# The first three channel chunks of a two-layer trunk kernel, taken together by pairs of k tiles

## The chip, the cores and the metric

One NeuronCore of one Trainium2 chip runs the whole program. The metric is the device time of one execution in microseconds. The kernel before takes 932.64 us (median of 3 runs, 932.36 to 933.33).

## What is computed

A decoder trunk of two layers over 256 positions and a model width of 1024, all in float32. The change touches only the opening of the first layer: an RMS norm and the first columns of one wide projection.

```python
h = rms_norm(x, norm_mix_g[i])          # x * rsqrt(mean(x*x) + 1e-6) * g
proj = h @ w_in                          # 1024 x 7960
(z, xbc, dt_raw, r_q, ...) = jnp.split(proj, idx, axis=-1)
xbc = jax.nn.silu(causal_dwconv(xbc, ssm_conv_w, ssm_conv_b))
...                                      # three token mixers, gates, w_out, then a gated MLP
```

## The kernel before

Float32 products are made of three rounded products: every weight and every activation is split into a high part and a low part, and TensorE adds high x high, high x low and low x high. A weight arrives in pieces of 128 partitions (`piece`, L167): a DMA on SyncE's queue into one of 4 `raw` buffers (L176), a cast on ScalarE that gives the high part `whi` (L183), a subtraction on VectorE that gives the low part `wlo` (L184). There are 6 buffers each of `whi` and `wlo`. Pieces are asked for 5 ahead of their use (`LOOK`); the dictionary `before` holds work that is put ahead of a given piece.

The activation is x itself, transposed, in 8 k tiles of 128 channels by 256 positions. It is loaded in 4 pairs of k tiles (`FirstNorm.ahead`, L340), each pair put ahead of one of pieces 1 to 4. ScalarE multiplies a k tile by the norm's gain and rounds it (`slot_h`, L302), VectorE makes the rest (`slot_l`, L303). The norm's other factor, one over the root mean square of each position, is not needed for the matmuls; it is multiplied in afterwards. It is made as follows: ScalarE squares the pairs (L348), GpSimd adds them up (L350, L354), TensorE sums over partitions (L358), VectorE takes the inverse root by 11 small operations (`rsqrt`, L284 to L289) and spreads it on a diagonal (L319), TensorE turns that into a row for all partitions (L322), ScalarE copies it out as `r_bc` (L324).

The first layer's matmuls start with three channel chunks of `xbc` of 256 columns each (chunks 2, 0, 1), each with 8 k tiles and 6 matmuls for a k tile, so 48 matmuls a chunk. Chunks 2 and 0 run interleaved (`chan_two`, in the order `LATE`), then chunk 1 (`chan_major`), then 16 matmuls of a narrow chunk (`narrow`, L256 and L260), then `z` (`tok_major`, L274 to L276). The results lie in PSUM tiles `mm`, of which there are 4. Each is freed when VectorE has multiplied it by `r_bc`: L459 in `take_xbc` for a channel chunk, L475 in `take_small` for the narrow one. `z` needs two `mm` tiles.

Ahead of all this, 5 matmuls of ones (`WARM`, L1065, 10 passes) keep TensorE at work while nothing has been loaded.

The order on each engine is that of a planner which follows the program's order of priority as far as its own estimate of readiness lets it; the queues then run in that fixed order. Side work (`spawn`) is advanced after a given number of `yield`s of the main stream, by the constants `N` and `W`.

Of the kernel before, what the change touches and what calls it, by code (L numbers as in the profile page):

```python
# [9 lines left out]
F32 = mybir.dt.float32  # L10
# [3 lines left out]
ALU = mybir.AluOpType  # L14
# [3 lines left out]
P = 128  # L18
D = 1024
T = 256  # L20
L = 2
KT = D // P
# [12 lines left out]

WARM = 5

LATE = (0, 2, 8, 10, 4, 12, 6, 14)

N = (3, 8, 3, 5, 3, 2)  # L40

# [13 lines left out]
PO = {}  # L55
_at = 0
# [6 lines left out]
PIECE = 1024  # L63
FIRST = 512
REST = 9
X_AT = 40
NFIRST = 2
RAW_BUFS = 4
# [51 lines left out]
for _l in range(L):  # L120
    for _n, (_kind, _j, _w) in enumerate(PLAN):
        _step = FIRST if _l == 0 and _n < NFIRST else PIECE
        PIECE_AT[_l, _kind, _j] = len(PIECES), _step
        PIECES += [(_l, _n, _o, min(_step, _w - _o)) for _o in range(0, _w, _step)]


@with_exitstack
def hybrid_trunk(ctx: ExitStack, tc: tile.TileContext, xT_in, x_in, wall, par, wa2, cst, phase, dret, fin, gbias, out):
    nc = tc.nc
# [9 lines left out]
    xt = cpool.tile([P, 2, D], F32, name="xt")  # L139
    params = [cpool.tile([P, NP], F32, name=f"par{l}") for l in range(L)]  # L140
    cs = cpool.tile([P, NC_CONST], F32, name="cs")
    ident = cs[:, CO_ID:CO_ID + P]
# [45 lines left out]
    def weight(l, kind, idx, k, cols):  # L188

        o = k * cols  # L190
        p, step = PIECE_AT[l, kind, idx]
        c = slice(o % step, o % step + cols)
        return (a[:, c] for a in piece(p + o // step))

# [54 lines left out]
    def narrow(l, act):  # L249

        ah, al = act
        acc = mm_tile()
        both = piece(PIECE_AT[l, "small", 0][0])[0].rearrange("p (k c) -> p k c", c=P)
# [73 lines left out]
    class FirstNorm(Norm):  # L327
# [9 lines left out]
        def ahead(self, j):  # L337
            o = 2 * (j % 2)
            x = self.x[j // 2][:, o:o + 2, :]
            nc.sync.dma_start(x, xT_in[:, 2 * j:2 * j + 2, :])  # L340
            for i in range(2):
                k = 2 * j + i
                split_scaled(self.slot[0][:, k, :], self.slot[1][:, k, :], x[:, i, :], self.g[:, k:k + 1])

        def square(self, j):
            sq = self.acc if j == 0 else t_main()
            o = 2 * (j % 2)
            nc.scalar.activation(two(sq), self.x[j // 2][:, o:o + 2, :], AF.Square)  # L348
# [557 lines left out]
    def layer(l, norm):  # L906

        mx = Mixers(l, norm)
        x_act = slots[0]
# [7 lines left out]

        yield from chan_two(l, "xbc", (2, 0), x_act, take)
        acc = yield from chan_major(l, "xbc", 1, x_act)
        mx.take_xbc(1, acc)  # L920
        yield
        mx.take_small(narrow(l, x_act))
        ssm = spawn(mx.ssm(), 1)
# [135 lines left out]
    def stream():  # L1059
        norm = FirstNorm(params[0][:, PO["mix_g"]:PO["mix_g"] + 8], slots[0])  # L1060

# [4 lines left out]

        def rest_ahead():
# [4 lines left out]
            for j in range(4):  # L1072
                norm.square(j)
# [18 lines left out]
def _lay_weights(i):  # L1092
# [4 lines left out]
    def put(l, kind, j, w):  # L1097
        k = w.shape[0] // P
        w = w.reshape(k, P, -1).transpose(1, 0, 2).reshape(P, -1)
        p, step = PIECE_AT[l, kind, j]  # L1100
        for o in range(0, w.shape[1], step):
            wall[p + o // step, :, :min(step, w.shape[1] - o)] = w[:, o:o + step]

# [102 lines left out]
```

## Time and profile before

| | before |
|---|---|
| time of 3 runs, us | 932.64 (932.36 to 933.33) |
| time of the profiled execution, us | 932.3 |
| its span from first to last instruction, us | 930.5 |
| TensorE matmul busy in it | 914.5 us, 98% |
| VectorE busy | 712.9 us, 77% |
| ScalarE busy | 506.8 us, 54% |

The span leaves out 1.8 us that lie around the instructions. Times in the rows are microseconds from the start of the span. A busy TensorE is not TensorE at its peak: it counts as busy at half clock as well, and the ends of matmuls are modelled, so the distance between the starts of two matmuls says more than the duration of one.

### The profile page before, as it was taken

To read this page: it belongs to the slowest core of one execution; us is meant where nothing else is said; L and a number is where in the kernel's file an instruction comes from. 1 tells how busy PE (TensorE), PEld (TensorE's weight loads), DVE (VectorE), ACT (ScalarE), POOL (GpSimd) and SP (SyncE) were. 2 spreads that over 40 slices of the span, in tenths; PEclk is the share of its full clock that TensorE was granted. 3 is DMA by queue.
4 is the path that set the end of the run, shared out by engine and by line. 5 is a ranking of instruction groups with operands and counts; after the bars stand their busy time and mean duration, and the time that the engine had idled before them with its cause. 6 is when DMAs were issued, how large, how long until landed. Compare 5 with 4: busy or idle time off the path is not lost.

```text
span 930.5 us, 14996 instructions
## 1 busy us (share of the span) xinstructions
PE 914.5 (98%) x5726; PEld 816.1 (88%) x5726; DVE 712.9 (77%) x1111; ACT 506.8 (54%) x748; POOL 78.4 (8%) x74
## 2 busy tenths in 40 slices
PE   8999999999999999999999999999999999999995
PEld 7879889888889999999898898888888999999994
DVE  6976888576768887787799578777667697777775
ACT  6765454454456555555566635554545575555552
POOL 3032200003200000000002131000120000000001
PEclk9999999999999999999999999999999999999998
DMA  7775655556655656555466556444665566555531
GB/s 255 276 243 166 219 172 170 152 162 210 201 181 161 202 183 186 188 192 181 147 186 183 198 168 218 158 139 156 206 212 194 169 188 189 190 183 184 183 109 46
DMA packets 51288, 169.94 MB, mean 183 GB/s; under 512 B 5968, under 2 KB 8336, under 8 KB 51088
## 3 DMA queue, kind: packets, MB, share of 16 engines
q1 hardware_dynamic: 50928, 168.46, 56.3%
q8 instruction: 45, 0.74, 0.3%
q10 hardware_dynamic: 288, 0.52, 0.2%
q14 instruction: 27, 0.22, 0.1%
HBM read 165.81 MB, written 1.05 MB: 179 GB/s over the span
## 4 chain that ended last, share of the span: by engine, by line
PE 94%; DVE 3%; ACT 1%; DMA 1%; issue 0%; SPq 0%; ACTq 0%
PE mm L227 13%; PE mm L228 13%; PE mm L229 13%; PE mm L274 12%; PE mm L275 12%; PE mm L276 12%; PE mx L1025 4%; PE mx L1024 4%; PE mx L1026 4%; PE mx L555 2%; DVE wlo L184 1%; PE mx L558 1%; DVE xbc L466 1%; PE mx L542 1%; DMA x_t<-x_t 1%; PE mx L726 1%
## 5 line engine op out<-in xcount | busy, mean ns | idle before, releaser
L184 DVE TENSOR_TENSOR wlo<-raw,whi 128x1024 fp32r<-128x1024 f32 (+1 forms) x300 | 377.6, 1261 | 123.6 <-ACT whi L183 120.6
L183 ACT CAST whi<-raw 128x1024 fp32r<-128x1024 f32 (+1 forms) x302 | 311.7, 1034 | 266.4 <-PE mm L276 109.3
L227 PE MATMUL mm<-slot_h,whi 128*128 128x256 f32 x992 | 282.4, 285 | 2.2 <-ACT slot_h L302 2.2
L228 PE MATMUL mm<-slot_l,whi 128*128 128x256 f32 x992 | 281.5, 284 | 0.1
L229 PE MATMUL mm<-slot_h,wlo 128*128 128x256 f32 x992 | 281.5, 284 | 0.0
L274 PE MATMUL mm<-whi,slot_h 128*128 128x512 f32 x512 | 203.9, 398 | 0.0
L275 PE MATMUL mm<-wlo,slot_h 128*128 128x512 f32 x512 | 200.4, 391 | 0.0
L276 PE MATMUL mm<-whi,slot_l 128*128 128x512 f32 x512 | 200.3, 391 | 0.0
L227 PEld LDWEIGHTS mm<-slot_h,whi 128*128 128x128 f32 x992 | 190.5, 192 | 4.9 <-ACT slot_h L302 2.6
L228 PEld LDWEIGHTS mm<-slot_l,whi 128*128 128x128 f32 x992 | 190.7, 192 | 2.1 <-DVE slot_l L303 0.3
L229 PEld LDWEIGHTS mm<-slot_h,wlo 128*128 128x128 f32 x992 | 190.7, 192 | 0.1
L274 PEld LDWEIGHTS mm<-whi,slot_h 128*128 128x128 f32 x512 | 96.2, 188 | 20.6 <-issue 0.7
L276 PEld LDWEIGHTS mm<-whi,slot_l 128*128 128x128 f32 x512 | 96.1, 188 | 20.3
L275 PEld LDWEIGHTS mm<-wlo,slot_h 128*128 128x128 f32 x512 | 96.3, 188 | 18.7
L1014 DVE SCALAR_TENSOR_TENSOR tm<-tm,par 128x255 f32<-128x255 f32 (+1 forms) x176 | 73.6, 478 | 0.7 <-ACT tm L1012 0.7
L1024 PE MATMUL mx<-whi,slot_h 128*128 128x512 f32 x176 | 69.1, 392 | 0.0
L1025 PE MATMUL mx<-wlo,slot_h 128*128 128x512 f32 x176 | 69.0, 392 | 0.0
L1026 PE MATMUL mx<-whi,slot_l 128*128 128x512 f32 x176 | 68.5, 389 | 0.0
L1012 ACT ACTIVATE tm<-tm,par 128x256 f32<-128x256 f32 x88 | 48.0, 592 | 4.3 <-DVE tm L1007 4.3
L1007 DVE TENSOR_TENSOR tm<-mm,r_bc 128x512 f32<-128x512 f32 x44 | 30.4, 690 | 23.1 <-PE mm L229 23.1
L1018 ACT CAST slot_h<-tm 128x256 fp32r<-128x256 f32 x44 | 17.9, 406 | 49.1 <-DVE tm L1017 49.0
L1026 PEld LDWEIGHTS mx<-whi,slot_l 128*128 128x128 f32 x176 | 33.1, 188 | 7.1
(193 smaller groups left out, 758.6 us busy)
## 6 DMA issues: line engine op xcount, KB each, us to landing
raw<-w_all SPq DMA_DIRECT2D x292, 512.0 KB, 3.5
gate_b<-gate_b SPq DMA_DIRECT2D x12, 256.0 KB, 3.5
st<-ret_decay SPq DMA_DIRECT2D x8, 384.0 KB, 3.8
raw<-w_all SPq DMA_DIRECT2D x10, 256.0 KB, 3.9
x_t<-x_t SPq DMA_DIRECT2D x4, 256.0 KB, 5.8
xt<-x_tok SPq DMA_DIRECT2D x1, 1024.0 KB, 6.3
r_c<-q SPq DMA_DIRECT2D x16, 64.0 KB, 2.0
r_d<-q SPq DMA_DIRECT2D x16, 64.0 KB, 2.0
```

What stands on the lines that cost most here:

```text
L183: nc.scalar.copy(h_out, r_in)
L184: nc.vector.tensor_tensor(l_out, r_in, h_out.bitcast(F32), ALU.subtract)
L227: nc.tensor.matmul(o, lhsT=wh[:, c], rhs=ah[:, k, :], start=first, stop=False)
L228: nc.tensor.matmul(o, lhsT=wh[:, c], rhs=al[:, k, :], start=False, stop=False)
L229: nc.tensor.matmul(o, lhsT=wl[:, c], rhs=ah[:, k, :], start=False, stop=last)
L274: nc.tensor.matmul(acc[t], lhsT=ah[:, k, c], rhs=wh, start=first, stop=False)
L275: nc.tensor.matmul(acc[t], lhsT=ah[:, k, c], rhs=wl, start=False, stop=False)
L276: nc.tensor.matmul(acc[t], lhsT=al[:, k, c], rhs=wh, start=False, stop=last)
L1014: nc.vector.scalar_tensor_tensor(a[:, d:], u[:, :T - d], mx.pc("fconv_w", 3 * ct + 2 - d), a[:, d:], ALU.mult, ALU.add)
L1024: nc.tensor.matmul(o, lhsT=ah[:, a, tok], rhs=wh, start=first, stop=False)
L1025: nc.tensor.matmul(o, lhsT=ah[:, a, tok], rhs=wl, start=False, stop=False)
L1026: nc.tensor.matmul(o, lhsT=al[:, a, tok], rhs=wh, start=False, stop=last)
```

## The change

- The three channel chunks of the first layer run together. Their weights come in 12 pieces of 512 columns (a pair of k tiles each), in the order in which they are used: the first pair of k tiles of chunks 2, 0 and 1, then the second pair, and so on. Three `mm` tiles are held until all 144 matmuls and the narrow chunk are done; only then `finish(factor)`, `take_small` and `take_xbc` follow.
- The pair of k tiles 0 of x is put ahead of piece 0, on ScalarE's DMA queue; the other pairs ahead of pieces 3, 6 and 9, on SyncE's.
- The norm's gain for the first layer comes as a small array of its own (`first_g`, 8 columns) on ScalarE's queue. The layer's parameters move from the head of SyncE's queue to just ahead of piece 8, and the constants to ahead of piece 11.
- The squares are put ahead of pieces 4, 7, 10 and 12. The last addition of squares and the closing sum move from GpSimd to VectorE.
- The object `Mixers` of the first layer is made after the second pair of k tiles; `WARM` goes from 5 to 6, `N[0]` from 3 to 2, `N[3]` from 5 to 8.

```diff
-WARM = 5
+WARM = 6
-N = (3, 8, 3, 5, 3, 2)
+N = (2, 8, 3, 8, 3, 2)
-REST = 9
+REST = 13
-NFIRST = 2
+NFIRST = 3
...
+    _cuts = [(_n, _o) for _o in range(0, PLAN[0][2], FIRST) for _n in range(NFIRST)] if _l == 0 else []
+    _cuts += [(_n, _o) for _n in range(NFIRST if _l == 0 else 0, len(PLAN)) for _o in range(0, PLAN[_n][2], PIECE)]
...
-            nc.sync.dma_start(x, xT_in[:, 2 * j:2 * j + 2, :])
+            (nc.sync if j else nc.scalar).dma_start(x, xT_in[:, 2 * j:2 * j + 2, :])
...
-                nc.gpsimd.tensor_tensor(self.acc, self.acc, sq, ALU.add)
+                (nc.vector if j == 3 else nc.gpsimd).tensor_tensor(self.acc, self.acc, sq, ALU.add)
...
-            nc.gpsimd.tensor_tensor(s1, self.acc[:, :T], self.acc[:, T:], ALU.add)
+            nc.vector.tensor_tensor(s1, self.acc[:, :T], self.acc[:, T:], ALU.add)
...
+            acc = [mm_tile() for _ in range(3)]
+            for k in range(0, KT, 2):
+                for i, b in enumerate((2, 0, 1)):
+                    chan_steps(l, "xbc", b, x_act, acc[i], (k, k + 1))
+                    yield
+                if k == 2:
+                    mx = Mixers(l, norm)
+            small = narrow(l, x_act)
+            yield
+            finish(factor)
+            mx.take_small(small)
+            for i, b in enumerate((2, 0, 1)):
+                mx.take_xbc(b, acc[i])
...
-        before.update({q + 1: lambda j=q: norm.ahead(j) for q in range(4)})
-        before[REST] = rest_ahead
-        nc.sync.dma_start(params[0], par[0])
+        before.update({3 * q: lambda j=q: norm.ahead(j) for q in range(4)})
+        before.update({3 * q + (4 if q < 3 else 3): lambda j=q: norm.square(j) for q in range(4)})
+        before[8] = lambda: nc.sync.dma_start(params[0], par[0])
+        before[11] = constants
+        before[REST] = rest_ahead
+        nc.scalar.dma_start(first_g, fg)
```

## Rows read from the trace of the kernel before

**Rows 1.** The page: busy time, share of the span, instructions of two engines.
```profile
PE 914.5 (98%) x5726; PEld 816.1 (88%) x5726; DVE 712.9 (77%) x1111; ACT 506.8 (54%) x748; POOL 78.4 (8%) x74
```
**Rows 2.** All waits of TensorE in the span: us in total, times, longest us.
```profile
PE mm L227 <- ACT slot_h L302: 2.2, 1, 2.2
...
PE mx L593 <- DVE da L584: 0.8, 1, 0.8
```
**Rows 3.** Instructions of TensorE in order of time: start us, us, line, what.
```profile
1.10 4.14 PE L1065 MATMUL mx<-ones 128*128 128x256 f32 x10 [1.10 <-POOL ones L150]
7.40 0.38 PE L227 MATMUL mm<-slot_h,whi 128*128 128x256 f32 x1 [2.16 <-ACT slot_h L302]
...
8.24 0.41 PE L229 MATMUL mm<-slot_h,wlo 128*128 128x256 f32 x1
...
11.44 0.28 PE L229 MATMUL mm<-slot_h,wlo 128*128 128x256 f32 x1
```
**Rows 4.** Busy us of each engine in three stretches, granted clock, DMA share, GB/s.
```profile
4.59:8.00 3.41, 1.11 (x5) 0.46 (x3) 1.31 (x3) 1.16 (x3) 0.00 (x0) 1.00 0.87 278
8.00:11.42 3.42, 3.42 (x16) 3.42 (x17) 3.21 (x7) 3.42 (x9) 0.00 (x0) 0.50 0.92 327
51.50:54.90 3.40, 2.69 (x12) 1.88 (x11) 3.36 (x4) 2.12 (x3) 1.90 (x1) 1.00 0.94 311
```
**Rows 5.** DMA issues of SyncE's queue in order of time.
```profile
0.74 0.39 SPq L1080 DMA_DIRECT2D par<-params  x1
1.18 0.42 SPq L176 DMA_DIRECT2D raw<-w_all  x1
1.64 0.43 SPq L340 DMA_DIRECT2D x_t<-x_t  x1
```
**Rows 6.** Issue to landing of the first x_t, then of the first raw (0 to 2).
```profile
DMA to landing us min/median/max: 5.2/5.2/5.2
DMA to landing us min/median/max: 2.7/2.7/2.7
```
**Rows 7.** Instructions of ScalarE in order of time.
```profile
0.74 1.28 ACT L441 ACT_TABLE_LOAD   x1 [0.74 <-PEq L1198]
3.94 0.62 ACT L183 CAST whi<-raw 128x512 fp32r<-128x512 f32 x1 [0.79 <-DMA raw<-w_all]
6.84 0.91 ACT L302 ACTIVATE slot_h<-x_t,par 128x256 fp32r<-128x256 f32 x2 [2.28 <-DMA x_t<-x_t]
25.80 0.37 ACT L324 COPY r_bc<-mx 128x256 f32<-128x256 f32 x1 [1.73 <-PE mx L322]
```
**Rows 8.** Instructions of TensorE from the norm's sum to z.
```profile
19.47 0.50 PE L358 MATMUL mx<-ones,sq 128*128 128x1 f32 x4
...
25.18 0.59 PE L322 MATMUL mx<-dg,ones 128*128 128x256 f32 x2
...
25.72 0.28 PE L227 MATMUL mm<-slot_h,whi 128*128 128x256 f32 x1
...
27.52 0.28 PE L260 MATMUL mm<-slot_h,whi 128*128 128x256 f32 x1
...
29.38 0.40 PE L274 MATMUL mm<-whi,slot_h 128*128 128x512 f32 x1
```
**Rows 9.** Instructions of VectorE in the same stretch and after it.
```profile
22.63 1.23 DVE L184 TENSOR_TENSOR wlo<-raw,whi 128x1024 fp32r<-128x1024 f32 x1
...
24.44 0.48 DVE L319 TENSOR_SCALAR dg<-cs,rs_y 128x128 f32<-128x128 f32 x2
...
26.21 0.69 DVE L459 TENSOR_TENSOR tm<-mm,r_bc 128x512 f32<-128x512 f32 x1 [0.16 <-ACT r_bc L324]
...
37.64 0.41 DVE L475 TENSOR_TENSOR small<-mm,r_bc 128x256 f32<-128x256 f32 x1
```
**Rows 10.** Instructions of GpSimd: the squares added up, and their closing sum.
```profile
13.37 4.75 POOL L350 TENSOR_TENSOR sqacc<-sqacc,tm 128x512 f32<-128x512 f32 x3 [10.07 <-ACT tm L348]
18.20 1.07 POOL L354 TENSOR_TENSOR sq<-sqacc 128x256 f32<-128x256 f32 x1
```

More of the change, by code (lines that the diff above doesn't have):

```diff
@@ L121, with hybrid_trunk @@
     for _n, (_kind, _j, _w) in enumerate(PLAN):
-        _step = FIRST if _l == 0 and _n < NFIRST else PIECE
-        PIECE_AT[_l, _kind, _j] = len(PIECES), _step
-        PIECES += [(_l, _n, _o, min(_step, _w - _o)) for _o in range(0, _w, _step)]
+        PIECE_AT[_l, _kind, _j] = [], FIRST if _l == 0 and _n < NFIRST else PIECE
+    _cuts = [(_n, _o) for _o in range(0, PLAN[0][2], FIRST) for _n in range(NFIRST)] if _l == 0 else []
+    _cuts += [(_n, _o) for _n in range(NFIRST if _l == 0 else 0, len(PLAN)) for _o in range(0, PLAN[_n][2], PIECE)]
+    for _n, _o in _cuts:
+        _kind, _j, _w = PLAN[_n]
+        _at, _step = PIECE_AT[_l, _kind, _j]
+        _at.append(len(PIECES))
+        PIECES.append((_l, _n, _o, min(_step, _w - _o)))
 @with_exitstack
-def hybrid_trunk(ctx: ExitStack, tc: tile.TileContext, xT_in, x_in, wall, par, wa2, cst, phase, dret, fin, gbias, out):
+def hybrid_trunk(ctx: ExitStack, tc: tile.TileContext, xT_in, x_in, wall, fg, par, wa2, cst, phase, dret, fin, gbias, out):
     nc = tc.nc
@@ L140, in hybrid_trunk @@
     params = [cpool.tile([P, NP], F32, name=f"par{l}") for l in range(L)]
+    first_g = cpool.tile([P, KT], F32, name="first_g")
     cs = cpool.tile([P, NC_CONST], F32, name="cs")
@@ L190, in weight @@
         o = k * cols
-        p, step = PIECE_AT[l, kind, idx]
+        at, step = PIECE_AT[l, kind, idx]
         c = slice(o % step, o % step + cols)
-        return (a[:, c] for a in piece(p + o // step))
+        return (a[:, c] for a in piece(at[o // step]))
     def mm_tile():
@@ L252, in narrow @@
         acc = mm_tile()
-        both = piece(PIECE_AT[l, "small", 0][0])[0].rearrange("p (k c) -> p k c", c=P)
+        both = piece(PIECE_AT[l, "small", 0][0][0])[0].rearrange("p (k c) -> p k c", c=P)
         for k in range(KT):
@@ L906, in layer @@
     def layer(l, norm):
-        mx = Mixers(l, norm)
+        mx = Mixers(l, norm) if l else None
         x_act = slots[0]
@@ L916, in take @@
             mx.take_xbc(b, acc)
[L918 to L922, printed above, removed]
+        if l:
+            yield from chan_two(l, "xbc", (2, 0), x_act, take)
+            acc = yield from chan_major(l, "xbc", 1, x_act)
+            mx.take_xbc(1, acc)
+            yield
+            mx.take_small(narrow(l, x_act))
+        else:
+            acc = [mm_tile() for _ in range(3)]
[6 more added lines that the diff above has]
+            small = narrow(l, x_act)
+            yield
+            finish(factor)
+            mx.take_small(small)
+            for i, b in enumerate((2, 0, 1)):
+                mx.take_xbc(b, acc[i])
         ssm = spawn(mx.ssm(), 1)
@@ L1059, in stream @@
     def stream():
-        norm = FirstNorm(params[0][:, PO["mix_g"]:PO["mix_g"] + 8], slots[0])
+        norm = FirstNorm(first_g, slots[0])
         cold = mx_tile()
@@ L1065, in stream, with constants @@
             nc.tensor.matmul(cold[:, :T], lhsT=ones[:, :P], rhs=ones, start=True, stop=True)
-        def rest_ahead():
+        def constants():
             nc.sync.dma_start(cs, cst)
@@ L1071, in rest_ahead @@
                 nc.vector.tensor_tensor(o, ident[:n, :8], ident[:n, p:p + 8], ALU.add)
-            for j in range(4):
-                norm.square(j)
+        def rest_ahead():
             for l in range(1, L):
                 nc.sync.dma_start(params[l], par[l])
-        before.update({q + 1: lambda j=q: norm.ahead(j) for q in range(4)})
+        before.update({3 * q: lambda j=q: norm.ahead(j) for q in range(4)})
[3 more added lines that the diff above has]
+        before[REST] = rest_ahead
         before[X_AT] = lambda: nc.sync.dma_start(xt, x_in)
-        before[REST] = rest_ahead
-        nc.sync.dma_start(params[0], par[0])
+        nc.scalar.dma_start(first_g, fg)
         piece(0)
@@ L1099, in put @@
         w = w.reshape(k, P, -1).transpose(1, 0, 2).reshape(P, -1)
-        p, step = PIECE_AT[l, kind, j]
-        for o in range(0, w.shape[1], step):
-            wall[p + o // step, :, :min(step, w.shape[1] - o)] = w[:, o:o + step]
+        at, step = PIECE_AT[l, kind, j]
+        for p, o in zip(at, range(0, w.shape[1], step)):
+            wall[p, :, :min(step, w.shape[1] - o)] = w[:, o:o + step]
     for l in range(L):
@@ L1189 @@
         "w_all": _lay_weights(i),
+        "first_g": np.ascontiguousarray(i["norm_mix_g"][0].reshape(KT, P).T),
         "params": _lay_params(i),
```

## The prediction

> **What bounds the kernel now.** I read the engines' busy shares first, then TensorE's waits, then its instructions in order of time, and last the other engines at the places where TensorE waits. TensorE is busy for 914.5 of 930.5 us [rows 1], and the list of its waits names only two places between the first product and the last: 2.2 us before the first product, for `slot_h` on ScalarE, and 0.8 us for `da` of the first layer's SSM [rows 2]. So the end moves by what TensorE's own stream gains or loses, and the change can act only in the first 30 us. There two things cost time. One is the idle stretch: the warm-up ends at 1.10 + 4.14 = 5.24 and the first product starts at 7.40 [rows 3]. The other is not in the list of waits: the granted clock is 0.50 (1.2 instead of 2.4 GHz) from 8.00 to 11.42, after a stretch in which TensorE was busy for 1.11 of 3.41 us [rows 4]. From the start at 8.24 to the one at 11.44 there are 15 matmuls [rows 3], so 3.20 / 15 = 0.213 us each; later, from 25.72 to 27.52, 15 matmuls take 1.80 us, 0.120 each [rows 8]. The slow stretch costs 15 x 0.093 = 1.40 us.
>
> The start hangs on x. The first pair of x is issued third on SyncE's queue, at 1.64 [rows 5], and lands 5.2 us later [rows 6]; the first weights, issued at 1.18, took 2.7 and were cast at 3.94. `slot_h` starts at 6.84 [rows 7], the first product 0.56 us after that [rows 3].
>
> **The change, part by part.** The reference for the sum is the profiled execution: 932.3 us, a span of 930.5 and 1.8 around it. The median of the runs is 932.64, 0.34 above it. I take the difference from the median. What a run of this kernel can be told apart by is about 0.2%, 1.87 us.
>
> (1) First x on ScalarE's queue, parameters out of the way. `first_g` stands ahead of it there, so x is second, as the first weights were on SyncE's: issue at about 1.18 instead of 1.64. How long it takes with two queues at work, no row shows. The bounds are the two landings of rows 6: 2.7 us (landing 3.9) and 5.2 us (landing 6.4). The first product would follow 0.56 us later, at 4.5 to 6.9. It can't start before the warm-up is over: one more warm-up matmul is two passes, and two such passes cost TensorE 0.42 us at full clock (L322: from 25.18 to 25.72, less one matmul of 0.12) [rows 8], so 5.24 + 0.42 = 5.66. Before, x had the parameters and the first weights ahead of it in its one queue; now it shares only with weights, and I place the landing at 5.1, nearer to the middle of the bounds, and the first product at 5.7. Gain 7.40 - 5.7 = **1.7 us** (0.5 to 1.7). The table load on ScalarE (1.28 us, from 0.74, [rows 7]) now belongs to the first `slot_h`; behind the two DMA issues it ends by 3.0 and is hidden by x's flight. If it stood ahead of them, x would leave 1.3 us later, within the same bounds for the start.
>
> (2) The half clock. With products from 5.7 on, TensorE is idle for next to nothing between 4.59 and 8.00. In the only other stretch with an idle piece, 51.50 to 54.90, it is busy for 2.69 of 3.40 us and the clock stays at 1.00 [rows 4]. So the slow stretch goes: gain **1.4 us** (0 if x comes at the late bound: the idle time is then 6.9 - 5.66 = 1.3 us, a busy share between the two rows).
>
> (3) Three chunks together. Same 144 + 16 matmuls, fed at 3 pieces and one pair of x for 36 x 0.12 = 4.3 us: that is 1 MB, 243 GB/s, below the 327 of 8.00 to 11.42 [rows 4]. ScalarE needs 3 casts of 0.62 and 0.91 for x, and about 0.62 for a square: 3.4 us, under 4.3. VectorE's share is alike. I cost the feeding at nothing; the buffers hold some two to three pieces in hand, and a late piece would show as a wait of L227 at up to 1 us each.
>
> The price is at the end of the three chunks. Before, the norm's row (L322) ran inside chunk 1: TensorE lost only 0.42 us there, went on until 27.52, did the narrow chunk until 29.38 and found the first `mm` tile long free (L459 started at 26.21) [rows 8, 9]. Now three chunks and the narrow chunk hold all 4 `mm` tiles, and none comes free before `r_bc`. L322 stands behind the narrow chunk, and nothing else is left for TensorE. From L322's start to that of `r_bc` it is 25.80 - 25.18 = 0.62, then 0.37 for the copy [rows 7], then `take_small` 0.41 [rows 9], which comes first in the program: 0.62 + 0.37 + 0.04 + 0.41 + 0.06 = 1.50 us to `z`, if `z` may take the narrow chunk's tile. If it has to wait for the tile of chunk 2, L459's 0.69 come on top, less 0.07 of overlap: 2.11. I take 1.50, since the narrow chunk's tile is freed first. Net of the 0.42 that L322 cost before: **loss 1.1 us** (1.1 to 1.7).
>
> L322 must also be ready by then. Before, it took 25.18 - 19.47 = 5.7 us from L358 to L322 [rows 8], in which VectorE put at least two weight subtractions of up to 1.23 us between the parts of the chain [rows 9]. Now L358 stands after the tenth of twelve groups; behind it are 0.36 of its own, two groups of 1.44 and the narrow chunk's 1.86: 5.1 us of cover. With one subtraction in between I get 4.5: no wait. With two, 0.6 us (bounds 0 to 0.6). The sum of squares must be there as well: on GpSimd three additions took 4.75, 1.58 each, and the closing one 1.07 [rows 10]; the last of each go to VectorE, where a 512-column operation takes 0.69 and a 256-column one 0.41 [rows 9]. It is 1.5 us shorter, and VectorE pays 1.1 us in a stretch in which it has 2.1 of 3.41 us free at the start, 4.59 to 8.00 [rows 4]; if that cover is gone, a subtraction is 1.1 us later, and two pieces are still in hand.
>
> (4) The rest. The parameters and constants come later on SyncE's queue, each passed by weights only; `take_xbc` needs them at some 26 us, ten later than they land. Two more, smaller pieces cost SyncE two issues of 0.42. Cost nothing.
>
> (5) The wait for `da` (0.8 us, [rows 2]). VectorE takes 10 us of `take_xbc` after `r_bc`, then the SSM's chain. `r_bc` comes at about the same time as before, 5.7 + 20.2 + 0.6 = 26.5 against 25.80, but VectorE can have two or three subtractions of `z` behind it by then. Bounds: 0.8 gained to 1.3 lost; nearest to no change, taken at 0.
>
> Sum: 1.7 + 1.4 - 1.1 = 2.0 us. `z` would start at 29.38 - 2.0 = 27.4, and the time is 932.64 - 2.0 = **930.6 us** (930.3 for an execution like the profiled one).
>
> **A rule against it.** What the rows show is that x, third in its queue, took nearly twice as long as the weights two places ahead [rows 6]. The Trainium skill says under Trainium Kernel Development and Optimization, Key Constraints, that DMAs issued from SyncE's and ScalarE's queues run on the same 16 DMA engines and interleave, so that issuing from several engines saves only issue time. By that rule x would gain its place (0.46 us) and nothing more; no row here has two queues at work at the start.
>
> **The rivals.**
> - A, as above: 930.6, between 930.0 and 931.5. For it: the rows of the start. 0.42.
> - B, the norm's row or `da` costs less: the planner puts L322 among the narrow chunk, or the wait for `da` goes as well. 0.8 to 1.1 us better: 929.6 (928.7 to 930.2). 0.21.
> - C, the idle piece before `z` costs the clock. It is 1.1 to 2.3 us long; before, 2.16 us of idleness came ahead of half clock and about 0.8 us did not [rows 3, 4]. Another 1.4 us: 932.0, with the longer wait for the tile 932.6. 0.17.
> - D, x still lands 5.2 us after its issue, since HBM and not the queue is slow then. First product at 6.94: gain 0.46 of 7.40, the half clock stays, the loss before `z` stays 1.1: 933.3. With L459 and the wait for L322 (0.6 + 0.6) and a second stretch at half clock (1.4) it is 935.9. It decides from a landing after about 6.0 on: then idleness before the first product is over 0.9 us. For it: the rule above. Against it: the moved 130 KB. 0.14.
> - E, VectorE falls behind after `r_bc`, and TensorE waits longer for `da` than it does now: up to 1.3 us more, 931.9. 0.06.
>
> **How the numbers follow.** Faster by over 0.2% means under 930.77: 0.26 of A and all of B, 0.47. Slower, over 934.5: the worse part of D and a little of E, 0.09. The rest, 0.44, lies within. Range: from B's lower end to D's plain case, 928.8 to 933.4.
>
> **What would show it.** Right: the first product before 6.0, no granted clock of 0.50 up to 20 us, an idle piece of TensorE of about 1 us between L322 and L274, `z` at 27.4. Wrong: `slot_h` still waiting for x after 6, a half clock behind `z`'s start, or L227 waiting for pieces.

## The result

The changed kernel is slower: 939.94 us (938.93 to 941.35, 6 runs) against 932.32 us for the kernel before, a ratio of 1.0079 (95% interval 1.0068 to 1.0090). The forecast was 930.6 us with 933.4 as its upper end. The profiled execution of the changed kernel took 941.35 us with a span of 939.6, 9.1 us more than the 930.5 before. It was the slowest of the six; the medians are 7.6 us apart.

All of TensorE's waits after the change (us in total, times, longest us); before there were 2.2 us at the start and 0.8 us for `da` [rows 2]:

```profile
PE mx L328 <- DVE dg L325: 5.5, 1, 5.5
PE mm L280 <- DVE small L481: 3.0, 1, 3.0
PE mm L233 <- ACT slot_h L308: 1.2, 1, 1.2
PE mx L1087 <- POOL ones L156: 1.1, 1, 1.1
```

Lines have moved by 6 (by 7 in the kernels below that hold work back), that of the warm-up by 22: L328 is the norm's row (L322 before), L280 the first product of `z` (L274), L233 the first product (L227), L481 is `take_small` (L475). The two upper waits are new, the one for `da` is gone. The places in TensorE's order of time (start us, us, line, operation, idle time before it and what ended it):

```profile
1.10 4.89 PE L1087 MATMUL mx<-ones 128*128 128x256 f32 x12 [1.10 <-POOL ones L156]
7.24 0.38 PE L233 MATMUL mm<-slot_h,whi 128*128 128x256 f32 x1 [1.25 <-ACT slot_h L308]
...
25.69 0.28 PE L266 MATMUL mm<-slot_h,whi 128*128 128x256 f32 x1
...
33.23 1.22 PE L328 MATMUL mx<-dg,ones 128*128 128x256 f32 x2 [5.51 <-DVE dg L325]
...
37.48 0.80 PE L280 MATMUL mm<-whi,slot_h 128*128 128x512 f32 x1 [3.02 <-DVE small L481]
```

The first product comes at 7.24 and not at 5.7. The narrow chunk begins at 25.69 where it began at 27.52 [rows 8]: 1.83 us won. Then TensorE stands still, and `z` begins at 37.48 instead of 29.38 [rows 8]. Four stretches of TensorE (us, busy us and instructions, granted clock, DMA share, GB/s) show what the clock did:

```profile
8.00:11.40 3.40, 3.40 (x30) 1.00 1.03 352
28.00:32.00 4.00, 0.00 (x0) 1.00 0.87 294
37.48:42.80 5.32, 5.32 (x13) 0.50 0.95 369
42.80:48.12 5.32, 5.32 (x27) 1.00 0.38 128
```

The half clock behind the first product [rows 4] is gone, as forecast. A longer one has come behind the idle time: from 32.56 to 42.80 the granted clock was 0.50 (1.2 GHz), and in the first 5.32 us of `z` TensorE did 13 matmuls where it did 27 in the next 5.32 (four of these small ones of 8 columns).

**Where the 9 us are made.** VectorE from the first step of the norm to `take_small`:

```profile
23.82 0.15 DVE L290 TENSOR_SCALAR rs_v<-mx 128x2 f32<-128x2 f32 x1
25.86 1.23 DVE L190 TENSOR_TENSOR wlo<-raw,whi 128x1024 fp32r<-128x1024 f32 x1 [1.89 <-ACT whi L189]
27.00 0.16 DVE L291 TENSOR_SCALAR rs_y<-rs_v 128x2 int32<-128x2 int32 x1
...
27.39 0.16 DVE L294 SCALAR_TENSOR_TENSOR rs_a<-rs_a,rs_v 128x2 f32<-128x2 f32 x1
27.87 1.23 DVE L190 TENSOR_TENSOR wlo<-raw,whi 128x1024 fp32r<-128x1024 f32 x1 [0.32 <-ACT whi L189]
29.01 0.15 DVE L295 SCALAR_TENSOR_TENSOR rs_y<-rs_a,rs_y 128x2 f32<-128x2 f32 x1
...
29.69 1.23 DVE L190 TENSOR_TENSOR wlo<-raw,whi 128x1024 fp32r<-128x1024 f32 x1
...
31.30 1.23 DVE L190 TENSOR_TENSOR wlo<-raw,whi 128x1024 fp32r<-128x1024 f32 x1
...
32.70 0.47 DVE L325 TENSOR_SCALAR dg<-cs,rs_y 128x128 f32<-128x128 f32 x2
33.09 1.22 DVE L190 TENSOR_TENSOR wlo<-raw,whi 128x1024 fp32r<-128x1024 f32 x1
35.86 1.22 DVE L190 TENSOR_TENSOR wlo<-raw,whi 128x1024 fp32r<-128x1024 f32 x1 [1.55 <-ACT whi L189]
37.01 0.42 DVE L481 TENSOR_TENSOR small<-mm,r_bc 128x256 f32<-128x256 f32 x1
```

The steps of the norm take 0.16 us each and follow one another every 0.20 us where nothing is between them (27.00 to 27.39 holds three). Here four weight subtractions of `z`'s pieces stand between them and two more between `dg` and `take_small`. VectorE takes its instructions in the written order, so `rs_y` at 27.00, ready since 23.97, stood 3 us behind a subtraction that was itself waiting. For what, ScalarE's rows say:

```profile
24.78 1.05 ACT L189 CAST whi<-raw 128x1024 fp32r<-128x1024 f32 x1 [1.56 <-DMA raw<-w_all]
26.79 1.05 ACT L189 CAST whi<-raw 128x1024 fp32r<-128x1024 f32 x1 [0.96 <-DMA raw<-w_all]
28.61 1.04 ACT L189 CAST whi<-raw 128x1024 fp32r<-128x1024 f32 x1 [0.78 <-DMA raw<-w_all]
...
34.79 1.04 ACT L189 CAST whi<-raw 128x1024 fp32r<-128x1024 f32 x1 [2.17 <-DMA raw<-w_all]
35.74 0.37 ACT L330 COPY r_bc<-mx 128x256 f32<-128x256 f32 x1
```

Each cast waits for its weights to land. `r_bc` has no reason of its own to be late: its input was there when L328 ended (34.45 by the row above), but it stands behind the cast of 34.79, which waited for a DMA. So the order of three engines had become one line: DMA, cast, subtraction, step of the norm.

### The profile page after: what moved, and what is told of

Its sections match the earlier page's. It is cut to its first block, busy times and chain, and to the rows that moved or that the text cites. A ratio compares the mean times of both kernels' runs of the same rounds, so it can differ in the third digit from the quotient of the medians.

```text
span 939.6 us, 15017 instructions
## 1 busy us (share of the span) xinstructions
PE 917.0 (98%) x5728; PEld 817.5 (87%) x5728; DVE 712.6 (76%) x1115; ACT 507.2 (54%) x750; POOL 76.6 (8%) x72
## 4 chain that ended last, share of the span: by engine, by line
PE 94%; DMA 3%; DVE 2%; ACT 1%; issue 0%; ACTq 0%
PE mm L280 13%; PE mm L281 13%; PE mm L282 13%; PE mm L233 12%; PE mm L234 12%; PE mm L235 12%; PE mx L1046 4%; PE mx L1047 4%; PE mx L1048 4%; DMA raw<-w_all 2%; PE mx L561 2%; PE mx L564 1%; DVE wlo L190 1%; PE mx L548 1%; DMA x_t<-x_t 1%; PE mx L732 1%
## 5 line engine op out<-in xcount | busy, mean ns | idle before, releaser
L233 PE MATMUL mm<-slot_h,whi 128*128 128x256 f32 x992 | 281.9, 284 | 1.2 <-ACT slot_h L308 1.2
L280 PE MATMUL mm<-whi,slot_h 128*128 128x512 f32 x512 | 205.2, 401 | 3.0 <-DVE small L481 3.0
L233 PEld LDWEIGHTS mm<-slot_h,whi 128*128 128x128 f32 x992 | 190.0, 192 | 3.9 <-ACT slot_h L308 1.6
L280 PEld LDWEIGHTS mm<-whi,slot_h 128*128 128x128 f32 x512 | 96.9, 189 | 24.2 <-DVE small L481 3.7
```

The lines of the kernel that those rows point to most:

```text
L233: nc.tensor.matmul(o, lhsT=wh[:, c], rhs=ah[:, k, :], start=first, stop=False)
L280: nc.tensor.matmul(acc[t], lhsT=ah[:, k, c], rhs=wh, start=first, stop=False)
```

## The experiments

The theory: work that fills VectorE's and ScalarE's queues and hangs on DMAs stands in the written order ahead of the norm's steps and results; TensorE has nothing else to do, and its idle time costs the clock as well. The rivals: the norm starts too late in the new order; the supply of weights holds everything; the loss lies in the start. Ratios are to the kernel before, timed beside each, with 95% intervals.

| kernel | us | ratio |
|---|---|---|
| the change | 939.94 | 1.0079 (1.0068 to 1.0090) |
| hold_one | 936.31 | 1.0036 (1.0022 to 1.0050) |
| hold_two | 933.47 | 1.0004 (0.9995 to 1.0013) |
| start_alone | 932.64 | 0.9999 (0.9987 to 1.0011) |
| chunks_alone | 934.91 | 1.0022 (1.0011 to 1.0032) |
| warm9 | 934.29 | 1.0009 (0.9995 to 1.0022) |
| warm9_later | 940.39 | 1.0080 (1.0058 to 1.0102) |
| x_first | 933.39 | 1.0010 (0.9999 to 1.0021) |
| hold_two_x_first | 933.77 | 1.0008 (0.9998 to 1.0017) |
| stat_early | 936.22 | 1.0033 (1.0021 to 1.0045) |
| hold_two_stat_early | 933.95 | 1.0007 (0.9999 to 1.0016) |
| hold_two_da_early | 933.32 | 1.0003 (0.9992 to 1.0015) |
| da_later | 938.81 | 1.0071 (1.0046 to 1.0096) |
| pool_three | 937.62 | 1.0047 (1.0029 to 1.0064) |
| pool_six | 939.99 | 1.0074 (1.0050 to 1.0097) |
| chunks_pool | 936.61 | 1.0035 (1.0023 to 1.0048) |
| hold_two_old_start | 931.41 | 0.9977 (0.9964 to 0.9989) |

### Hold the subtractions back, in two steps

**hold_one** prepares no piece of `z` and the gates until `dg` is written.

```diff
+    cap = [13]
...
-        while len(loaded) < min(p + 1 + LOOK, len(PIECES)):
+        while len(loaded) < min(p + 1 + LOOK, len(PIECES), *cap):
...
             finish(factor)
+            cap.clear()
+            with tc.issue_after(norm.dg_made):
+                piece(12)
             mx.take_small(small)
```

> The changed kernel with one thing altered: the weight subtractions of z and of the first gate piece are traced behind the norm's chain and tied on VectorE behind its last step (L325, dg), so that none stands between the eleven steps of rsqrt. Theory (order): the fixed order of VectorE put five subtractions, each waiting for its own DMA, into the chain; without them dg is ready before the narrow chunk ends (27.6) and the wait of L328 falls from 5.5 us to under 0.5. Four casts and four subtractions now stand ahead of r_bc and of take_small instead, so z starts at 31 to 33 instead of 37.5: 933 to 937 us. Rival (weights): the weights simply come too late with the parameters and constants among them, whatever the order; then the wait moves but z still starts after 36: 938 to 941. Rival (tiles): holding all four mm tiles until r_bc is the cost in itself; then L328 is on time and z still starts some 2 us after it, 930 to 933.

VectorE from `dg` on in hold_one:

```profile
26.43 0.47 DVE L326 TENSOR_SCALAR dg<-cs,rs_y 128x128 f32<-128x128 f32 x2
26.85 2.36 DVE L191 TENSOR_TENSOR wlo<-raw,whi 128x1024 fp32r<-128x1024 f32 x2
30.38 2.48 DVE L191 TENSOR_TENSOR wlo<-raw,whi 128x1024 fp32r<-128x1024 f32 x2 [1.17 <-ACT whi L190]
32.78 0.42 DVE L482 TENSOR_TENSOR small<-mm,r_bc 128x256 f32<-128x256 f32 x1
```

`dg` comes at 26.43 instead of 32.70 and the wait for it is gone. But the four subtractions now all stand between `dg` and `take_small`: TensorE waits 4.7 us for `small`, `z` begins at 33.25, the granted clock is 0.50 from 32.99 to 36.41. The wait had moved from the first result of the norm to the second.

**hold_two** lets one piece of `z` follow `dg`, and ties the casts of the others behind `r_bc` and their subtractions behind `take_small`.

```diff
-            cap.clear()
+            cap[:] = [14]
             with tc.issue_after(norm.dg_made):
                 piece(12)
             mx.take_small(small)
+            cap.clear()
+            with tc.issue_after(norm.r_made), tc.issue_after(mx.small_made):
+                piece(12)
```

> As hold_one, and the casts of z's later pieces are tied behind r_bc on ScalarE, their subtractions behind take_small on VectorE; only z's first piece is converted earlier. Theory (order): the whole path is free, L328 starts at about 27.6, r_bc at 28.2, z at 29.0 to 29.7, against 29.38 in the kernel before; no half clock behind it: 930.5 to 933 us, level with the kernel before. Rival (weights): over 936. Rival (tiles): as the theory, with 1.4 to 2 us of idle TensorE between L328 and z left over.

TensorE in hold_two:

```profile
27.27 0.59 PE L329 MATMUL mx<-dg,ones 128*128 128x256 f32 x2
28.79 0.50 PE L281 MATMUL mm<-whi,slot_h 128*128 128x512 f32 x1 [0.92 <-DVE small L482]
```

From L329 to `z` it is 1.52 us, the 1.50 of the forecast's step (3), and `z` begins 0.6 us earlier than before the change. From 5.5 to 923 us the granted clock is 1.00. Of the 7.6 us that the change cost all but 0.7 are back (933.47 against 932.78 us of the kernel before beside it), with the start as the change has it. The first four pieces of 1024 columns land at 24.7, 26.7, 28.5 and 29.8 us in the change and at 24.5, 26.7, 28.2 and 29.5 in hold_two, the two behind them 1.4 and 1.9 us later in hold_two. `z` begins 8.7 us earlier all the same, so the supply of weights is not what held it back.

### The norm's sum two steps earlier

**stat_early** is the change with one number, `N[3]`, at 6 instead of 8; **hold_two_stat_early** is hold_two with the same. In both, and in hold_two_da_early, the sum is taken before the squares of the last two k tiles are added; they are left out of the norm.

```diff
-N = (2, 8, 3, 8, 3, 2)
+N = (2, 8, 3, 6, 3, 2)
```

> The changed kernel with one number of its schedule changed: the sum of squares and its product come two steps (two pairs of k tiles, some 2.6 us) earlier in the three chunks. VectorE's written order then has no weight subtraction among the steps of the norm, but four between dg and the product with r_bc. Theory 'subtractions that wait for their DMA stand in VectorE's order ahead of the norm's results': the wait of 5.5 us for dg goes, r_bc and the product with r_bc still stand behind four casts and four subtractions, z begins near 33 us as in hold_one (33.25), and the time is about 936 us. Rival 'the norm simply starts too late by a fixed amount': the wait for dg shrinks by 2.6 us to about 2.9 us, all else follows as before, and the time is about 937.3 us.

VectorE in stat_early:

```profile
22.43 0.69 DVE L190 TENSOR_TENSOR wlo<-raw,whi 128x512 fp32r<-128x512 f32 x1 [0.95 <-PE mm L234]
23.04 0.15 DVE L290 TENSOR_SCALAR rs_v<-mx 128x2 f32<-128x2 f32 x1
...
25.74 0.48 DVE L325 TENSOR_SCALAR dg<-cs,rs_y 128x128 f32<-128x128 f32 x2
26.85 2.49 DVE L190 TENSOR_TENSOR wlo<-raw,whi 128x1024 fp32r<-128x1024 f32 x2 [0.63 <-ACT whi L189]
29.73 2.48 DVE L190 TENSOR_TENSOR wlo<-raw,whi 128x1024 fp32r<-128x1024 f32 x2 [0.39 <-ACT whi L189]
32.13 0.42 DVE L481 TENSOR_TENSOR small<-mm,r_bc 128x256 f32<-128x256 f32 x1
```

The norm's sum on TensorE came 3.2 us earlier (19.03 against 22.27), its first step on VectorE only 0.8 us (23.04 against 23.82), because a subtraction that waited stands ahead of it again. What changed is the place of the four subtractions: none among the steps, four behind `dg`. The wait for `dg` is gone, the one for `small` is 4.9 us, `z` begins at 32.60 and the time is 936.2: hold_one's picture without holding anything back. The rival (an earlier norm, waits shorter by as much, 937.3 us) doesn't fit the waits.

> hold_two with the sum of squares and its product two steps (some 2.6 us) earlier. dg, r_bc and the product with r_bc come at least 1 us earlier, so that the 0.9 us in which TensorE stood still ahead of z in hold_two goes and z begins near 27.8 us (29.4 before the change). 'What TensorE gains stays': about 932.3 us against 933.5 us of hold_two. 'VectorE's line to da takes it back': da still begins at 55 us or 0.5 us earlier, the wait for it grows from 0.8 to about 1.5 us, and the time is 933.0 to 933.5 us.

Nothing was won: `dg` came at 25.61 (25.54 in hold_two), so the earlier sum brought no earlier `dg`, and in both kernels `dg` is written over 1 us before L329 starts (at 27.46 here, 27.27 in hold_two), which stands behind the narrow chunk. In hold_two `dg` is not what binds. In `z` TensorE waited twice, 0.8 and 1.1 us, for `take_xbc` (L466) to free a tile, where hold_two has one such wait of 0.7.

### Take the subtractions off VectorE

**pool_three** and **pool_six** are the change, **chunks_pool** is chunks_alone (below), with three or six of the subtractions on GpSimd; casts and DMAs keep their order.

```diff
-            nc.vector.tensor_tensor(l_out, r_in, h_out.bitcast(F32), ALU.subtract)
+            (nc.gpsimd if q in (13, 15, 17) else nc.vector).tensor_tensor(l_out, r_in, h_out.bitcast(F32), ALU.subtract)
```

(`13 <= q <= 18` in pool_six.)

> The changed kernel with the weight subtractions of every other one of z's first pieces (three in all) on GpSimd in place of VectorE; casts, DMAs and all else as they are. VectorE's order then has one subtraction among the steps of the norm in place of four, and one in place of two behind dg. Theory 'the subtractions stand in VectorE's queue, and each waits for its cast and its DMA': dg comes 3 us earlier or more (32.70 in the change), TensorE's two waits of 5.5 and 3.0 us shrink to about 2 and 2 us, z begins at 31 to 33 us in place of 37.5, and the time is 934 to 936 us. Rival 'the supply of weights or of the buffers holds everything back': GpSimd's additions took some 1.3 us for 512 columns, so its subtractions of 1024 take some 2.6 us; buffers come free later, and the time stays at 939 us or above.

> As pool_three, with the subtractions of z's first six pieces on GpSimd. VectorE then has none among the steps of the norm nor before the product with r_bc. Theory: dg near 26 us, no wait for it, the wait for small under 1.5 us (r_bc still behind a cast or two), z near 29 us; but six subtractions one behind the other on GpSimd take some 16 us where z asks for a piece every 2.7 us, so TensorE can wait for wlo in z, up to some 2 us; the time is 932.5 to 935 us. Rival (supply): above 938 us.

> chunks_alone (934.9 us) with the subtractions of three of z's first pieces on GpSimd. No subtraction stands among the steps of the norm here, two stand behind dg. Theory 'place in VectorE's queue': the wait for dg (1.5 us) goes, that for small shrinks from 2.8 to about 2 us, no half clock behind z, and the time is 931.5 to 933 us. If VectorE's line to da caps it, the wait for da comes back with 1 us or more and the time is near 933 us. Rival (supply): 934.9 us or more.

All three missed: the medians of 937.62, 939.99 and 936.61 us lie above the ranges of the theory, the last two in the ranges given for the supply. In pool_three TensorE still waited 5.4 us for `dg`, in pool_six 2.6; in chunks_pool that wait went and the one for `small` grew to 4.1. The rows show another reason than the supply. VectorE in pool_three:

```profile
27.52 2.22 DVE L190 TENSOR_TENSOR wlo<-raw,whi 128x1024 fp32r<-128x1024 f32 x1 [2.43 <-ACT whi L189]
29.67 2.29 DVE L295 SCALAR_TENSOR_TENSOR rs_y<-rs_a,rs_y 128x2 f32<-128x2 f32 x1
```

GpSimd in the same execution:

```profile
28.98 2.97 POOL L190 TENSOR_TENSOR wlo<-raw,whi 128x1024 fp32r<-128x1024 f32 x1 [0.32 <-ACT whi L189]
```

A step of the norm, 0.16 us wherever GpSimd has no subtraction, took 2.29 us while GpSimd's subtraction ran, to within 0.01 us of its end (29.67 + 2.29 = 31.96, 28.98 + 2.97 = 31.95). In chunks_pool the same step took 2.26 us from 24.93 and ended at 27.19 with GpSimd's subtraction (2.40 us from 24.79). In pool_six, where VectorE has no subtraction left before `take_small`, the two parts of `dg` took 4.79 us instead of 0.48 beside GpSimd's row of six, and six operations of `take_xbc` 8.26 us (2.45 in pool_three). The one part of the theory that could still be read: with one subtraction left among the steps, VectorE reached the step before it at 24.93 and went on at 27.52, having waited 2.43 us for the cast; the wait for `small` fell from 3.0 to 0.9 us in pool_three and pool_six. Since the move slowed VectorE in a new way, these three neither support the theory by their times nor speak for the supply.

### The two halves of the change apart

**start_alone** is the kernel before with the new start only: `first_g` and the first x on ScalarE's queue, the parameters behind the weights, six warm-up products.

```diff
-            nc.sync.dma_start(x, xT_in[:, 2 * j:2 * j + 2, :])
+            (nc.sync if j else nc.scalar).dma_start(x, xT_in[:, 2 * j:2 * j + 2, :])
...
-        nc.sync.dma_start(params[0], par[0])
+        nc.scalar.dma_start(first_g, fg)
```

> The kernel before, with the new start alone: first x and a small first_g on ScalarE's queue, the parameters behind the first x pairs, WARM 6; chunks and their order as before. If the new start is worth what the changed trace shows (first product at 7.24 instead of 7.40, no half clock), the gain is 0.16 + 1.4: 930.5 to 931.3 us, and no wait at r_bc. If the later parameters cost as much, 932 to 933.

First product at 7.17 (7.40 before), the half clock from 7.57 to 10.99 still there, the last product of the three chunks at 27.50 (27.40), the wait for `da` 1.4 us: no change in time. Six warm-up products did not keep the clock here; TensorE had been idle for 1.72 us. The start brought nothing and cost nothing.

**chunks_alone** is the change with the old start, and `WARM` 5.

```diff
-            (nc.sync if j else nc.scalar).dma_start(x, xT_in[:, 2 * j:2 * j + 2, :])
+            nc.sync.dma_start(x, xT_in[:, 2 * j:2 * j + 2, :])
...
-        before.update({3 * q: lambda j=q: norm.ahead(j) for q in range(4)})
+        before.update({(3 * q if q else 1): lambda j=q: norm.ahead(j) for q in range(4)})
...
-        nc.scalar.dma_start(first_g, fg)
+        nc.sync.dma_start(params[0], par[0])
```

> The changed kernel with the old start: first x on SyncE's queue behind the first weights, parameters ahead of all, WARM 5; the three chunks together, their pieces and the later work as in the change. Theory (order): here only two subtractions stand inside the chain and two behind it, by the program's order, so the wait of L328 is shorter than 5.5 us, 1 to 4, and the start is at half clock again: 934 to 940 us. If late parameters and constants were the cause, it would be at 932 to 934.

TensorE's waits in chunks_alone:

```profile
PE mm L280 <- DVE small L481: 2.8, 1, 2.8
PE mx L328 <- DVE dg L325: 1.5, 1, 1.5
```

The loss is in this half, but it is smaller, 2.1 us of time, with a half clock from 30.94 to 34.35: the planner put two subtractions among the steps here, not four, and two more behind `dg`. The two halves apart do not add up to the 7.6 us; the other 5.5 came only with the order that the planner wrote for both. The old start was the better one in this execution: x, third on SyncE's queue, landed 3.6 us after its issue and the first product came at 5.84. In the changed kernel, on ScalarE's queue, the rows of that tile read:

```profile
L346 ACTq DMA_DIRECT2D x_t<-x_t x1: 454/454/454, 1.2 to 1.2; - x1
...
DMA to landing us min/median/max: 5.4/5.4/5.4
```

The other profiled executions agree: nine with x on ScalarE's queue, issued at 1.2, took 5.2 to 5.6 us; seven with x third on SyncE's, issued at 1.6, took 3.1, 3.3, 3.6, 4.0, 4.3, 5.2 and 5.3. The kernel before [rows 6] was one of the two slowest.

### Is an earlier start worth anything?

Four kernels, all made from the one before, were to tell whether a gain at the start lasts: **warm9**, **warm9_later**, **da_later** (the product with `da` two token products later in these two; the latter with `WARM` 5), and **x_first** (x ahead of the first weights on SyncE's queue). The edits of warm9_later (warm9 has the first line of it, da_later the second), then of x_first:

```diff
-WARM = 5
+WARM = 9
...
-W = (4, 5, 4, 4, 1, 6, 5, 3, 5, 3, 3, 4, 3, 2, 6, 2, 6, 2, 4, 5, 8)
+W = (4, 6, 4, 4, 1, 6, 5, 3, 5, 3, 3, 4, 3, 2, 6, 2, 6, 2, 4, 5, 8)
```

```diff
-        before.update({q + 1: lambda j=q: norm.ahead(j) for q in range(4)})
+        before.update({(q + 1 if q else 0): lambda j=q: norm.ahead(j) for q in range(4)})
+        before[5] = lambda: nc.sync.dma_start(params[0], par[0])
...
-        nc.sync.dma_start(params[0], par[0])
+        nc.scalar.dma_start(first_g, fg)
```

> The kernel before with nine warm-up products in place of five, so that TensorE has no idle time ahead of the first product (2.16 us before) and nothing of the change. Both theories: no stretch at the half clock behind the first product (before 7.6 to 11.0 us), and the last product of the first three chunks ends about 1.4 us earlier. Theory 'what is gained at the start stays': the wait for da stays at about 0.8 us and the time falls by about 1.4 us, to 931.1 us. Theory 'VectorE's line of work from r_bc to da takes it back' (da began at 55.0 us before, at 55.8 and 55.5 us in two kernels whose start differed): da still begins near 55 us, the wait for it grows to about 2.2 us, and the time is that of the kernel before within 0.3 us.

> warm9 with the step that needs da put two token products later in the hand-written order. If VectorE's line to da takes the gain back, TensorE now has about 0.5 us more work ahead of that wait, which shrinks from about 2.2 us by as much, and the time falls by about 0.5 us, to 932.0 us. If the gain stays anyway, the wait is near 0.3 us here and the time is that of warm9 within 0.3 us.

> The kernel before with the one number of warm9_later that puts the product with da two token products later, and the start as it was. If the 2.4 us that warm9_later lost behind 100 us come from this number and not from the start, waits for tx of about 1.7 us stand here too and the time is 934 to 936 us. If they came from the start, the wait for da (0.8 us) shrinks to about 0.3 us here and the time is 932.0 us.

> The kernel before with only the order of the first loads changed: the first two k tiles of x lead SP's queue, ahead of the first weight, a small table of gains goes on ScalarE's queue, the parameters go behind the first five weight pieces; five warm-up products. If the early transfers are bound by the bytes that the DMA engines have moved (about 0.80 MB by 5 us in every kernel so far), not by the queue, x lands by about 4 to 5 us, the first product starts at 5.2 to 5.8 us (7.40 before), and no stretch at the half clock follows. The last product of the first three chunks then ends about 1.4 to 3 us earlier. 'What is gained at the start stays': 929.5 to 931.1 us. 'VectorE's line to da takes it back': the wait for da grows to 2 us or more, and the time falls by at most what that line starts earlier, to 931.5 to 932.5 us.

warm9 and x_first had no half clock behind the first product and gained nothing. In the order of before, the product with the norm's sum stands behind the 84th of the 144 products, and it began at 19.47, 19.46, 19.51 and 19.45 us in before, start_alone, warm9 and x_first, whose first products lay between 6.83 and 7.88; in x_first TensorE waited 1.1 us at 16.05 for a `wlo`, in warm9 the starts of its products show several gaps of 0.25 to 0.53 us in place of 0.12. What was gained at the start was gone by then; the causes differ, and I read no more from it than that. warm9 is also no clean test: the planner wrote one more subtraction ahead of the work behind `r_bc`, and TensorE waited 1.5 us for a `wlo` in `z`. The later place of `da` is what cost warm9_later its time: da_later has the old start and the same two waits of 1.7 us for `tx`, at 116 and 573 us. They make 3.4 us; the median of da_later, 938.81 us, lies 6.3 above the kernel before, outside the 934 to 936 us expected, and the rest is not explained.

**hold_two_x_first** is hold_two with x ahead on SyncE's queue and five warm-up products, **hold_two_da_early** is hold_two_stat_early with the SSM's first part begun two steps earlier, **hold_two_old_start** is hold_two with the old start (the edit of chunks_alone). The edit of hold_two_x_first, then that of hold_two_da_early:

```diff
-WARM = 6
+WARM = 5
...
-            (nc.sync if j else nc.scalar).dma_start(x, xT_in[:, 2 * j:2 * j + 2, :])
+            nc.sync.dma_start(x, xT_in[:, 2 * j:2 * j + 2, :])
```

```diff
-            yield W[0]
+            yield 2
...
                 nc.vector.tensor_tensor(da[:, 8 * t:8 * t + 8], dt[:, 8 * t:8 * t + 8], self.aneg, ALU.mult)
+            yield W[0] - 2
```

> hold_two (the change, with the weight subtractions and casts of later pieces held behind the steps of the norm) with the first two k tiles of x in front of SP's queue instead of on ScalarE's, and five warm-up products. If x in front of one queue lands by about 4 to 5 us, the first product starts near 5.5 us against 7.2 us in hold_two. The three chunks then end about 1.5 us earlier and the eleven steps of the norm, with no subtraction between them, start as much earlier: about 932.0 us against 933.5 us of hold_two, if nothing later takes it back; if VectorE's line to da does, the wait for da (0.8 us in hold_two) grows to about 2 us and the time stays at 933 to 933.5 us.

> hold_two_stat_early with the step that makes dt and da begun two steps earlier in the written order (the step itself cut in two, its first part moved). 'VectorE's line to da takes the gain back': da begins 2 us earlier or more, the wait of TensorE for it goes, and the time falls by about that wait, to 931.7 us or less. 'It was not da': the time stays that of hold_two_stat_early within 0.3 us or gets worse, with another wait in its place.

> hold_two with the start of the kernel before (parameters first, x behind the first weights on SP's queue, five warm-up products). If x lands about 3.6 us after its issue as in chunks_alone, the first product starts near 5.9 us, z near 27.5 us. 'The gain of the start stays': 932.0 us. 'VectorE's line to da takes it back': the wait for da, 0.8 us in hold_two, grows by the same 1.3 us and the time is that of hold_two, 933.5 us. If x lands 5.2 us after its issue, it is hold_two's time with the early half clock, 933.5 to 935 us.

In hold_two_x_first x landed at 4.3 us, and ScalarE was late instead:

```profile
4.42 1.28 ACT L309 ACT_TABLE_LOAD   x1 [4.42 <-DMA x_t<-x_t]
5.71 0.91 ACT L309 ACTIVATE slot_h<-x_t,first_g 128x256 fp32r<-128x256 f32 x2
6.53 1.64 ACT L190 CAST whi<-raw 128x512 fp32r<-128x512 f32 x3
```

With x as its first input ScalarE loaded its table only when x had landed, did `slot_h` next and cast the first weights last; the first product began at 7.18, 2.8 us after x was there, and the half clock came back. x_first has the same order from 4.07 on. In hold_two_da_early the wait for `da` went and 0.7 us for a `wlo` and 0.1 for `xbc` came in its place; its median lies 0.6 us below that of hold_two_stat_early, between what the two theories gave. hold_two_old_start is the version that beats both kernels. Its waits of TensorE:

```profile
PE mm L282 <- DVE wlo L191: 1.6, 1, 1.6
PE mx L1094 <- POOL ones L156: 1.1, 1, 1.1
PE mm L281 <- DVE small L482: 0.9, 1, 0.9
PE mx L600 <- DVE da L591: 0.3, 1, 0.3
```

x landed 3.1 us after its issue. The first product began at 5.30, 1.9 us ahead of hold_two's, `z` at 27.69, 1.1 us ahead, and the span is 0.94 us shorter (929.8 against 930.8). So in these two executions about half of the gain at the start lasts. By the medians, each against the kernel before beside it, the two kernels lie 2.2 us apart (hold_two 0.69 above it, this one 1.55 below), against the 1.9 us gained; what part lasts is not settled, for the landing of x differs between executions. The guess that the line of work to `da` takes all of it back was wrong, for the product with `da` came at 54.0 us here and `da` was waited for 0.3 us. What stays open is whether the 1.6 us for a `wlo` in `z` are the price of the earlier start; they weren't there in hold_two. More raw buffers, which would let the DMAs run further ahead, were not tried.

## Why the prediction was wrong

Counted on TensorE's starts, against the forecast of 1.7 + 1.4 - 1.1 = 2.0 us won:

| step | forecast, us | measured, us |
|---|---|---|
| (1) first product earlier | 1.7 won | 0.16 won (7.40 to 7.24) |
| (2) no half clock in the chunks | 1.4 won | 1.67 won (first product to narrow chunk: 20.12 to 18.45) |
| (3) narrow chunk's start to `z` | 1.1 lost, up to 1.7 | 9.93 lost (1.86 to 11.79) |
| half clock behind `z` (only in rival C) | 0 | about 2.5 lost (12 matmuls in 5.29 us, 37.48 to 42.77; before in 2.77, 29.38 to 32.15) |
| (5) wait for `da` | 0 | 0.8 won |

Measured, 9.93 + 2.5 lost and 0.16 + 1.67 + 0.8 won make 9.8 us lost, against 9.1 by the spans; the 0.7 between them I can't place. The forecast counted (3) net of the 0.42 us that the norm's row had cost among the chunks before; counted so, (3) lost 9.51 and (2) won 1.25.

- **Step (3) failed**, in one clause, on whether the norm's row is ready: "With one subtraction in between I get 4.5: no wait. With two, 0.6 us". There were four, and they cost not only their 1.2 us each but the waits for their casts and DMAs too. `dg` came 8.9 us after the chain's first step (23.82 to 32.70); with nothing in between it takes 2.2 (24.20 to 26.43 in hold_one). I had read the number of subtractions off the order of before, where the chain ran beside chunk 1, and took their number and their price as given. The order belongs to the planner, which wrote another for the new program (two in chunks_alone, none in stat_early). The other half of the same step was priced without any subtraction: L322 to `z` at 1.50. That is right when nothing stands in between (1.52 in hold_two); in the change it was 4.25.
- **Step (1) failed** at the landing of x, 5.1 us being taken for its time where it was 6.6. The bounds I gave (2.7 and 5.2 us after issue) held 5.4 almost; the reason for a value in the middle was wrong: "now it shares only with weights", as if the one queue had been its trouble. (The weights that it was compared with stood one place ahead of x in that queue, not two.) The trace shows the second weight piece, issued at the same 1.18, landing at 6.41 and x at 6.59. That is what the Trainium skill states under Trainium Kernel Development and Optimization, Key Constraints: SyncE's and ScalarE's queues are served by the same DMA engines, interleaved, and a second queue saves issue time only. The trace agrees with the rule. By rival D, with 0.14, x was to land 5.2 us after its issue; it took 5.4.
- **Step (2) was right**, though not by its reason, that next to no idle time would be left: TensorE was idle for 1.25 us before the first product and kept the clock. For idle time like this, 1.3 us at x's late bound, the forecast had allowed a gain of 0, so in part this was luck. start_alone, with six warm-up products as well, lost the clock after 1.72 us; no run varies the idle time alone.
- **Step (4) was right**: no product of the three chunks waited for a piece.
- **Step (5)**: taken at 0 within 0.8 won to 1.3 lost, it came to the favourable end, for the wrong reason: `z` was so late that `da` was ready.
- **Rivals.** C named the clock that was lost behind idle time, at 1.4 us, for an idle piece of 1.1 to 2.3 us. D's worst case, 935.9, was the nearest number, by other means. None had VectorE's queue ahead of `r_bc` as a cause of its own; D's worst case holds 0.6 us of it. E put VectorE's lateness behind `r_bc` only. Of the signs named for being wrong two came: `slot_h` waited for x until 6.68, and a half clock stood behind `z`'s start.

## What to carry to other kernels

When a change takes away the work that TensorE did during a latency chain, look at everything that stands in the chain's own queues, not at the chain's length: an in-order engine that has been given fill-in work hanging on DMAs makes the chain as slow as the DMAs. Hold such work back behind the chain's last result on each engine it passes (VectorE and ScalarE here), for holding it behind the first result only moves the wait. And take the time of a transfer at the start from several executions before a forecast rests on it.

## What the runs showed of the hardware

- The first x, third on one queue, landed 3.1 to 5.3 us after its issue in seven executions; on a second queue, with weights in flight on the first, 5.2 to 5.6 us in nine. One trace of before could not show that spread.
- VectorE beside GpSimd: an operation on 128x2 took 2.29 us, 0.16 otherwise, and ended with GpSimd's 128x1024 subtraction; the two parts of `dg` took 4.79 us instead of 0.48. In pool_three and chunks_pool the rows show VectorE held until GpSimd's instruction was over, to within 0.01 us. The Trainium skill states a means, under SBUF — State Buffer, SBUF: two separate sides: the two engines take turns at one pair of ports, each keeps it for a whole instruction, and a VectorE operation with two inputs in SBUF is among those that wait. The trace agrees for `rs_y`, which has two.
- The clock at the start: after idle times of 2.16 (before), 1.72 (start_alone) and 1.66 us (hold_two_x_first) the granted clock fell to 0.50 behind the first product; after 1.25 (the change), 1.10 (x_first) and 1.09 us (hold_two) it did not. With five warm-up products the clock was not always up by their end: in da_later the idle time was 0.51 us, and the first products, from 7.14 to 9.92, still followed one another at 0.21 us, the half rate. The profile's column of the granted clock reads 1.00 there, so at the start of a span the distances between starts are the surer sign.
